# Three modulation vectors of a diffusion trunk: products on GpSimd and sums on ScalarE in place of TensorE matmuls

## The chip, the cores and the metric

One core of a Trainium2 chip runs the whole program. The metric is the device time of one execution in microseconds, smaller being better. The engines are TensorE (PE, with its weight loads PEld), VectorE (DVE), ScalarE (ACT), GpSimd (POOL) and SyncE (SP), which here only issues DMAs.

## What is computed

Two layers, each an FFN, a mixer (latent attention beside a state-space branch S5) and another FFN, on 256 latent and 256 context tokens of 1024 channels. Each branch is normed, scaled and shifted ahead, and gated behind, by vectors of 1024 channels that come from a conditioning vector: nine per layer, for the latent and for the context tokens.

```python
mod_x = (silu(c) @ ada_w[l] + ada_b[l]).reshape(B, 9, 1, 1024)
mod_c = (silu(c_ctx) @ ada_w[l] + ada_b[l]).reshape(1, 9, 1, 1024)
sublayer_in  = rmsnorm(h, g_pre) * (1 + mod[:, 3*s + 1]) + mod[:, 3*s]
sublayer_out = h + weight * mod[:, 3*s + 2] * rmsnorm(y, g_post)
# branch s: 0 first FFN, 1 mixer, 2 second FFN
```

Vector 2 of a layer is so the gate behind the first FFN; 3 and 4 are shift and scale ahead of the mixer.

## The kernel before

All matmuls of the main path are made of three in fp32r: a weight tile of 128x512 is loaded (`raw`), ScalarE rounds it (`whi`), VectorE subtracts (`wlo`), and TensorE multiplies whi and wlo with the high and low parts of the activations (`hhi`/`hlo` behind a norm, `hi`/`lo` behind a gate). The FFN goes through its 22 blocks of hidden channels in four segments; the last part of the last segment is done for the 256 context tokens first and the latent ones next (h = 0, 1), eight output blocks of 15 matmuls each. Behind every block `close` (line 765) makes x², (G y)² and x·G y into a tile `tri` for the statistics: the squares and `y` scaled by the gate on ScalarE, the product x·y on GpSimd for blocks 0 to 5 (on VectorE for 6 and 7). TensorE adds their columns (`misc<-tri`), `Norm.chain` (line 2036) makes the norm's factors on VectorE, TensorE spreads them (`acc<-sp`), and `Norm.block` (line 2065) gives hhi and hlo, for which ScalarE needs the shift `B` and the scale `A`.

Beside this path S5's matrices of the layer are built (`s5_build`, line 1599): mostly VectorE products of 128x512 (`P`, `mt`, ...), then small matmuls (`acc<-P,c`, transposes `acc<-ident,mt`), ScalarE copies (`m`, `kb`) and stores to DRAM issued by GpSimd (`stg`, `kd`).

The 18 vectors come in three ways. `ada_first` (line 838) makes vectors 0 and 1 of layer 0 at the start, on TensorE. `ada_gen` (line 791) makes 2, 3 and 4 of layer 0: for each half of a vector eight pieces of 128x512 of ada_w are loaded (`aw`), each multiplied by the two conditioning vectors (32 columns, four matmuls a piece), copied to a row (`adr`), transposed and added to the bias: 48 pieces. `ada_rows` (line 864) makes the other 13 on VectorE, from rows of the transposed ada_w: each 128x512 tile `ar` is multiplied by the conditioning vector on all partitions (`crow`) and summed in one instruction.

```python
for j in range(4):
    nc.tensor.matmul(bank[32 * j:32 * j + 32], self.silu[:, kt, :], w[:, j * 128:(j + 1) * 128],
                     start=kt == 0, stop=kt == 7)
```

The order of the work is not that of the code. The class Recorder takes down all instructions with a time at which each is due, and `schedule` (line 379) orders each engine's queue by its own estimates. Work beside the path is a "filler": `add_filler` (line 627) records one step whenever the recorded time of the main path passes its next due time; what is marked lazy is put into idle time up to then. `need` (line 892) records the rest of a generator at once when a vector is wanted that is not there. All instructions are issued from one line of `emit` (line 576), so every row of the trace has L576.

Of the kernel before, what the change touches and what calls it, by code (L numbers as in the profile page):

```python
# [17 lines left out]
L = 2  # L18
# [4 lines left out]
LEAD = 6  # L23
# [11 lines left out]
ADA_ROWS = [(0, 5), (0, 6), (0, 7), (0, 8), (1, 0), (1, 1), (1, 2), (1, 3), (1, 4), (1, 5), (1, 6), (1, 7), (1, 8)]  # L35
ROWS_FROM, ROWS_PACE = 360000.0, 4.5
# [8 lines left out]
ADA_PACE = 12000.0  # L45
# [27 lines left out]
class View:  # L73
    """A part of an on-chip tile, as strides over [128 partitions, columns]."""
# [55 lines left out]
    def extent(self):  # L130
        """The first partition, the last, and the columns as bits."""
        p, c = divmod(self.offset(), self.root.cols)
        key = c, self.arr.shape[1:], self.arr.strides[1:]
        if key not in MASKS:
            at = np.array([c])
            for n, st in zip(*key[1:]):
                at = (at[:, None] + st * np.arange(n if st else 1)).reshape(-1)
            m = 0
            for x in at.tolist():
                m |= 1 << x  # L140
            MASKS[key] = m
        return p, p + self.arr.shape[0], MASKS[key]
# [14 lines left out]
class Root:  # L157
    """A tile: lasting, or one of a tag's buffers from its first write to its last use."""
# [18 lines left out]
class Scratch:  # L177
    """A part of a DRAM tensor, with what tells it from parts that other instructions use."""
# [41 lines left out]
class Recorder:  # L220
    """Records instructions, then issues them in the order of a list schedule.

    An instruction waits for those that it depends on and for its buffers; each engine takes the one that was
    recorded for the earliest time among those that can run.
    """
# [18 lines left out]
    # ---------------------------------------------------------------- tiles  # L244
# [14 lines left out]
    # ---------------------------------------------------------------- priorities  # L259
    @contextmanager  # L260
    def aside(self, late, pace=0.0, lazy=False):
        """Work beside the main path, as if recorded some time later, and by and by.

        Lazy work is for an engine's idle time, up to the time at which its result is needed.
        """
# [8 lines left out]
    # ---------------------------------------------------------------- recording  # L274
    def cost(self, eng, method, a, kw):
        """Time on the engine, in ns."""
# [101 lines left out]
    # ---------------------------------------------------------------- schedule  # L378
# [166 lines left out]
    def lacks(self, op):  # L545
        """A tile that the instruction is the first to use and that has to wait for a buffer, if there is one.

        A tile gets a buffer only if all that is still to come, in the order of the recording, then fits as well.
        """
# [29 lines left out]
class Trunk:  # L579
# [24 lines left out]
    # ---------------------------------------------------------------- storage  # L604
# [21 lines left out]
    # ---------------------------------------------------------------- fillers  # L626
    def add_filler(self, gen, interval, delay=0.0, late=0, pace=0.0, lazy=False):
        """A generator whose steps are recorded at intervals, with the priority of a later time.

        With a pace the intervals are that many times VectorE's work in a step.  # L630
        """
# [21 lines left out]
    # ---------------------------------------------------------------- weights  # L653
# [8 lines left out]
    def wget(self):  # L662
        """Loads and splits the weights that come next."""
# [14 lines left out]
    # ---------------------------------------------------------------- matmuls  # L678
# [20 lines left out]
    # ---------------------------------------------------------------- norms  # L699
    def part(self, t, h):  # L700
        """Half h of the tokens of a tile: 0 the context, 1 the latent ones, which an x-only tile holds alone."""
# [10 lines left out]
    def stat(self, r, q, n=1):  # L712
        """Adds a block's column sums to n regions of the statistics bank: 4 quadrants by 64 tokens."""
# [5 lines left out]
    def rsqrt(self, v, plain=False, wide=True, times=1.0, mask=None):  # L719
        """times/sqrt of [quadrant, token] rows: as they are, and with the tokens of other quadrants as zeros."""  # L720
# [28 lines left out]
    def rstd(self, r, width, n=1):  # L749
        """1/rms of the sums of squares in n regions from r on."""  # L750
# [4 lines left out]
    def spread(self, p, rows):  # L755
        """Rows of 64 tokens, one of each quadrant, to [128, 256 tokens] on every partition."""
# [8 lines left out]
    def close(self, l, s, i, h, y, src, fast, last=False):  # L765
        """Statistics of half h of block i of a branch's output: sums of src^2, y^2 and x y for y = G src."""
# [21 lines left out]
    # ---------------------------------------------------------------- modulation  # L788
    ADA_AHEAD = 4

    def ada_gen(self, units):
        """One step: one [128, 512] piece of ada_w for the two conditioning vectors."""
        nc = self.nc
        halves = [(l, m, h) for l, m in units for h in range(2)]
        pieces = [(*x, kt) for x in halves for kt in range(8)]
        tiles = {}
        nxt = 0

        def load(upto):
            nonlocal nxt  # L800
            while nxt < min(upto, len(pieces)):
                l, m, h, kt = pieces[nxt]
                w = self.rec.tile("slot", 512, F32, "aw")
                c = m * 1024 + h * 512
                nc.sync.dma_start(w, self.io["ada_w"][l, kt * 128:(kt + 1) * 128, c:c + 512])
                tiles[nxt] = w
                nxt += 1

        tail = []

        def finish(l, m, h, row):
            tp = self.aux()[:, 0:128]
            nc.tensor.transpose(tp, row, self.ident)
            c = m * 8 + h * 4
            nc.vector.tensor_tensor(_ap(self.mods[l], c * 2, [[2, 4], [1, 2]]), _ap(tp, 0, [[32, 4], [1, 2]]),
                                    _ap(self.adab, l * 72 + c, [[1, 4], [0, 2]]), op=ALU.add)
            if h == 1:
                self.have[l, m] = True

        for i, (l, m, h, kt) in enumerate(pieces):  # L820
            load(i + 1)
            if kt == 2 and tail:
                finish(*tail.pop())
            w = tiles.pop(i)
            if kt == 0:
                bank = self.acc()[:, 0:128]
            for j in range(4):
                nc.tensor.matmul(bank[32 * j:32 * j + 32], self.silu[:, kt, :], w[:, j * 128:(j + 1) * 128],
                                 start=kt == 0, stop=kt == 7)
            if kt == 7:  # L830
                row = self.sm(128, tag="adr")
                nc.scalar.activation(row, bank, AF.Copy)
                tail.append((l, m, h, row))
            yield
        finish(*tail.pop())
        yield

    def ada_first(self):
        """One step: a quarter of the channels of the two units that the first norm needs."""
# [23 lines left out]

    def ada_rows(self, units):
        """The same on the vector engine: one step gives 128 channels from their rows of the transposed ada_w."""
# [79 lines left out]
    def fill_ada(self, n):  # L945
        for _ in range(n):
            if next(self.ada, 0) == 0:
                return
# [1264 lines left out]
```

## Time and profile before

| | us |
|---|---|
| median of 3 runs | 2319.44 (2319.03 to 2321.52) |
| span of the profiled execution | 2323.8 |
| TensorE busy | 2275.3 |
| VectorE busy | 1870.1 |
| ScalarE busy | 1029.1 |
| GpSimd busy | 300.6 |

The page lists for the profiled execution its span, from the first instruction to the last, and no separate device time; it lies 4.4 us above the median. The matmuls are pipelined, so a matmul's own duration is longer than the distance to the next one. The first FFN of layer 0 ends and its mixer begins between 461 and 468 us; the profile's windows are cut there.

### The profile page before, as it was taken

The numbers are of one execution on the slowest core, as the hardware profiler recorded it, in microseconds if no ns is written. First come the engines' busy times: TensorE is split into PE (matmuls) and PEld (weight loads), VectorE is DVE, ScalarE is ACT, GpSimd is POOL, SyncE is SP. The second block draws the span as 40 slices with busy tenths as digits, with TensorE's granted clock in tenths as the row PEclk, the third lists the DMA queues.
The fourth block names the chain that finished last, engine by engine and source line by source line (L and its number), as shares of the span: only waits on it lengthen the run. The fifth ranks groups of instructions, "written<-read, shape, count | busy, mean of one in ns | idle before, by whom it ended". The sixth has DMA issues, their size and how long they took to land. (4 is left out here: it accounts for less than half of the span.)

```text
span 2323.8 us, 43733 instructions
## 1 busy us (share of the span) xinstructions
PE 2275.3 (98%) x15768; PEld 1947.8 (84%) x15768; DVE 1870.1 (80%) x4313; ACT 1029.1 (44%) x2050; POOL 300.6 (13%) x455
## 2 busy tenths in 40 slices
PE   8999999999999999999999999999999999998998
PEld 6887878887888888898888888888889898897997
DVE  4997788889889889699997899898557678877554
ACT  5332233653246644543222463333246446575452
POOL 0010111430100200200100131100004110312000
PEclk9999999999999999999999999999999999998999
DMA  9354556966874546243564645656445795673562
GB/s 318 97 162 147 170 186 202 350 194 197 295 256 148 162 147 226 69 123 111 163 197 125 206 148 161 206 191 227 155 137 161 244 299 174 174 258 120 178 195 88
DMA packets 237481, 428.06 MB, mean 184 GB/s; under 512 B 29488, under 2 KB 58032, under 8 KB 237264
## 3 DMA queue, kind: packets, MB, share of 16 engines
q1 hardware_dynamic: 213904, 350.79, 47.8%
q0 software_dynamic: 23360, 74.48, 9.1%
q8 instruction: 124, 2.03, 0.4%
q14 instruction: 93, 0.76, 0.1%
HBM read 366.56 MB, written 58.59 MB: 183 GB/s over the span
## 5 line engine op out<-in xcount | busy, mean ns | idle before, releaser
L576 PE MATMUL acc<-hhi,whi 128*128 128x256 f32 (+2 forms) x2112 | 717.1, 345 | 4.8 <-ACT hhi L576 4.1
L576 PE MATMUL acc<-hhi,wlo 128*128 128x256 f32 (+2 forms) x2112 | 707.6, 343 | 0.0
L576 PE MATMUL acc<-hlo,whi 128*128 128x256 f32 (+2 forms) x2112 | 699.9, 342 | 1.5 <-DVE hlo L576 1.5
L576 ACT ACTIVATE whi<-raw 128x512 fp32r<-128x512 f32 x802 | 476.0, 623 | 367.1 <-PE acc L576 157.8
L576 DVE TENSOR_TENSOR wlo<-raw,whi 128x512 fp32r<-128x512 f32 x802 | 529.6, 686 | 125.4 <-ACT whi L576 75.8
L576 PEld LDWEIGHTS acc<-hhi,whi 128*128 128x128 f32 (+1 forms) x2112 | 398.8, 190 | 56.9 <-ACT hhi L576 6.7
L576 PEld LDWEIGHTS acc<-hhi,wlo 128*128 128x128 f32 (+1 forms) x2112 | 398.9, 190 | 47.5 <-issue 0.6
L576 PEld LDWEIGHTS acc<-hlo,whi 128*128 128x128 f32 (+1 forms) x2112 | 390.3, 189 | 50.8 <-DVE hlo L576 2.8
L576 PE MATMUL acc<-hi,whi 128*128 128x512 f32 (+1 forms) x1144 | 392.4, 345 | 1.5 <-ACT hi L576 1.5
L576 PE MATMUL acc<-lo,whi 128*128 128x512 f32 (+1 forms) x1144 | 389.0, 341 | 0.0
L576 PE MATMUL acc<-hi,wlo 128*128 128x512 f32 (+1 forms) x1144 | 378.8, 343 | 0.6 <-DVE wlo L576 0.6
L576 PEld LDWEIGHTS acc<-hi,whi 128*128 128x128 f32 x1144 | 215.3, 189 | 32.4 <-issue 5.1
L576 PEld LDWEIGHTS acc<-hi,wlo 128*128 128x128 f32 x1144 | 214.3, 189 | 27.6 <-DVE wlo L576 1.8
L576 PEld LDWEIGHTS acc<-lo,whi 128*128 128x128 f32 x1144 | 215.6, 189 | 24.6 <-issue 0.3
L576 ACT ACTIVATE sg<-acc 128x512 f32<-128x512 f32 (+1 forms) x129 | 64.8, 503 | 252.2 <-PE acc L576 234.3
L576 ACT ACTIVATE hi<-sg 128x512 fp32r<-128x512 f32 (+1 forms) x113 | 60.4, 540 | 158.1 <-DVE sg L576 129.6
L576 DVE TENSOR_TENSOR sg<-sg,acc 128x512 f32<-128x512 f32 (+1 forms) x97 | 55.6, 574 | 90.4 <-ACT sg L576 63.4
L576 POOL TENSOR_TENSOR tri<-x,y 128x256 f32<-128x256 f32 x54 | 54.7, 1018 | 323.5 <-ACT y L576 296.1
L576 DVE CUSTOM_DVE_ANT_0 ar<-ar,crow,adab 128x512 f32<-128x512 f32 x104 | 77.6, 750 | 4.5 <-DMA ar<-in_ada_t_dram 4.5
L576 DVE TENSOR_TENSOR lo<-sg,hi 128x512 fp32r<-128x512 f32 (+1 forms) x113 | 66.0, 589 | 17.5 <-ACT hi L576 9.9
L576 DVE CUSTOM_DVE_ANT_0 ar<-ar,crow,ah 128x512 f32<-128x512 f32 x104 | 78.8, 758 | 1.5 <-DMA ar<-in_ada_t_dram 0.9
L576 POOL DMA_DIRECT2D stg<-P x64 | 34.8, 543 | 345.1 <-DVE P L576 345.1
(249 smaller groups left out, 3282.2 us busy)
## 6 DMA issues: line engine op xcount, KB each, us to landing
raw<-in_w_gu_dram SPq DMA_DIRECT2D x352, 256.0 KB, 3.2
ar<-in_ada_t_dram SPq DMA_DIRECT2D x208, 256.0 KB, 3.4
raw<-in_w_dn_dram SPq DMA_DIRECT2D x176, 256.0 KB, 3.2
raw<-in_w_sq_dram SPq DMA_DIRECT2D x128, 256.0 KB, 4.6
raw<-in_w_in_dram SPq DMA_DIRECT2D x112, 256.0 KB, 4.9
m1l<-stg SPq DMA_DIRECT2D x96, 256.0 KB, 5.0
aw<-in_ada_w_dram SPq DMA_DIRECT2D x80, 256.0 KB, 5.8
stg<-P POOLq DMA_DIRECT2D x64, 256.0 KB, 3.8
```

The source lines that it names most:

```text
L576: getattr(getattr(self.tc.nc, engine), method)(*[real(v) for v in a], **{k: real(v) for k, v in kw.items()})
```

## The change

`ada_gen` goes, and `ada_sums` takes its place for the same three vectors. A step makes 128 channels: two tiles `ar` of 128x512 from the transposed ada_w, each multiplied on GpSimd by the `crow` of the two conditioning vectors, and each product summed along its row by a ScalarE copy with an accumulator (`apart`). After eight steps VectorE adds the halves and the bias. So there are 4 products and 4 sums a step, 24 steps. The first step is due at 25 us of the main path's recorded time, the others 14.5 us apart. The `crow` tiles are loaded by this generator, earlier than before. The rest of the diff takes comments out.

```diff
-ADA_PACE = 12000.0
+ADA_SUMS = [(0, 2), (0, 3), (0, 4)]
+SUMS_FROM, SUMS_PACE = 25000.0, 14500.0
...
+    def ada_sums(self, units):
+        nc = self.nc
+        self.load_crow()
+        for u, (l, m) in enumerate(units):
+            part = self.const([128, 32], name="apart")
+            for b in range(8):
+                w = [self.blk(name="ar") for _ in range(2)]
+                for i in range(2):
+                    nc.sync.dma_start(w[i], self.io["ada_t"][len(ADA_ROWS) + u, b, :, i * 512:i * 512 + 512])
+                for r in (0, 1):
+                    for i in range(2):
+                        o = self.blk(name="aj") if r == 0 else w[i]
+                        c = 4 * b + 2 * r + i
+                        nc.gpsimd.tensor_tensor(o, w[i], self.crow[r][i], op=ALU.mult)
+                        nc.scalar.activation(o, o, AF.Copy, accum_out=part[:, c:c + 1])
+                yield
+            v = self.modv(l, m)
+            q = part.rearrange("p (b i) -> p b i", i=2)
+            nc.vector.tensor_tensor(v, q[:, :, 0], q[:, :, 1], op=ALU.add)
+            o = v.rearrange("p (b r) -> p b r", r=2)
+            bias = self.adab[:, l * 72 + m * 8:l * 72 + m * 8 + 8].unsqueeze(2).to_broadcast([128, 8, 2])
+            nc.vector.tensor_tensor(o, o, bias, op=ALU.add)
+            self.have[l, m] = True
+            yield
...
-        self.ada = self.ada_gen([(l, m) for l in range(L) for m in range(9) if (l, m) not in ADA_ROWS + [(0, 0), (0, 1)]])
+        self.ada = self.ada_sums(ADA_SUMS)
...
-        self.add_filler(self.ada, ADA_PACE, 2000.0, LATE_A, 0.0, True)
+        self.add_filler(self.ada, SUMS_PACE, SUMS_FROM, LATE_A, 0.0, True)
```

How the queues move is read from the order of the built programs. The numbers behind the names tell tiles apart within one program alone. GpSimd at the end of the first FFN, before: the products x·y of blocks 3 (context), 0, 4, 5, 1 to 5, between stores of S5's matrices.

```order
L576 TENSOR_TENSOR tri_4839<-x_87,y_1778 128x256
L576 DMA kd_99<-kb_4893 128x240
L576 DMA stg_101<-m_4904 128x512
L576 DMA stg_101<-m_4917 128x512
L576 DMA stg_101<-m_4931 128x512
L576 DMA stg_101<-m_4942 128x512
L576 TENSOR_TENSOR tri_4992<-x_84,y_1641 128x256
L576 TENSOR_TENSOR tri_5051<-x_88,y_1813 128x256
L576 TENSOR_TENSOR tri_5079<-x_89,y_1842 128x256
L576 TENSOR_TENSOR tri_5161<-x_85,y_1690 128x256
```

The same place in the changed program begins with these rows; `aj` and `ar` are products with `crow`, and behind the last row of the piece 16 more of them follow, the last being ar_4808.

```order
L577 TENSOR_TENSOR aj_4790<-ar_4498,crow_115 128x512
L577 TENSOR_TENSOR tri_4781<-x_88,y_1931 128x256
L577 TENSOR_TENSOR aj_4838<-ar_4526,crow_114 128x512
L577 TENSOR_TENSOR aj_4859<-ar_4534,crow_115 128x512
L577 TENSOR_TENSOR ar_4526<-ar_4526,crow_112 128x512
L577 TENSOR_TENSOR ar_4534<-ar_4534,crow_113 128x512
```

Behind ar_4808 stands the product x·y of block 5 for the context tokens, tri_4788, and behind it the tri for the latent ones:

```order
L577 DMA kd_99<-kb_5231 128x240
L577 TENSOR_TENSOR tri_4788<-x_89,y_1967 128x256
L577 DMA stg_101<-m_5069 128x512
L577 DMA stg_101<-m_5114 128x512
L577 TENSOR_TENSOR tri_4947<-x_84,y_1734 128x256
```

Further on, behind the rest of the tri and two x of the norm, come stores, and at their end the 22nd product, the last of the three vectors:

```order
L577 DMA stg_101<-m_5425 128x512
L577 DMA stg_101<-m_4872 128x512
L577 DMA stg_101<-m_4883 128x512
L577 DMA kd_99<-kb_4901 128x240
L577 DMA stg_101<-m_5271 128x512
L577 TENSOR_TENSOR ar_4498<-ar_4498,crow_113 128x512
```

Twenty-two products have come into this part of the queue; tri_4788 stands behind 21 of them, and ar_4498 behind all the stores.

ScalarE at the mixer's first norm, before: two tri, the last whi, and the first hhi.

```order
L576 ACTIVATE tri_5391<-y_1918 128x256
L576 ACTIVATE tri_5391<-y_1918,cG_112 128x256
L576 ACTIVATE whi_5400<-raw_5076 128x512
L576 ACTIVATE hhi_5411<-pn_5398,c_75,cA_113 128x8x32
L576 ACTIVATE pn_5416<-pn_5398,c_75,cA_113 128x256
```

And in the changed program, where `apart` is the sums' tile:

```order
L577 ACTIVATE tri_5359<-y_1967 128x256
L577 ACTIVATE whi_5389<-raw_5146 128x512
L577 ACTIVATE whi_5397<-raw_5157 128x512
L577 ACTIVATE whi_5407<-raw_5167 128x512
L577 ACTIVATE whi_5418<-raw_5175 128x512
L577 ACTIVATE m_5425<-acc_5226 128x512
L577 ACTIVATE ar_4498,apart_118<-ar_4498 128x512
L577 ACTIVATE hhi_5503<-pn_5438,c_75,cA_120 128x8x32
```

The last sum has come to stand directly ahead of the first hhi.

## Rows read from the trace of the kernel before

**Rows 1.** The page, its first part: busy us, share of the span, instructions.
```profile
PE 2275.3 (98%) x15768; PEld 1947.8 (84%) x15768; DVE 1870.1 (80%) x4313; ACT 1029.1 (44%) x2050; POOL 300.6 (13%) x455
```

**Rows 2.** Windows: stretch, its length, busy us by engine, clock, DMA share, GB/s.
```profile
50.00:200.00 150.00, 150.00 (x742) 127.58 (x741) 137.90 (x361) 56.58 (x101) 10.82 (x20) 1.00 0.47 152
200.00:400.00 200.00, 199.80 (x1139) 159.91 (x1138) 161.44 (x274) 60.11 (x105) 23.72 (x44) 1.00 0.53 170
400.00:468.00 68.00, 65.61 (x758) 56.21 (x757) 58.84 (x142) 42.56 (x95) 26.34 (x38) 0.98 0.96 343
```

**Rows 3.** Windows of tile aw, of tile adr; TensorE's timeline around pieces of aw.
```profile
100.00:460.00 360.00, 20.35 (x384) 10.87 (x384) 1.00 0.59 196
...
100.00:460.00 360.00, 1.69 (x6) 0.84 (x6) 1.65 (x6) 1.00 0.59 196
...
421.22 1.52 PE L576 MATMUL acc<-aw,c 128*32 128x128 f32 x48
422.55 0.51 PE L576 MATMUL misc<-tri,c 128*32 128x192 f32 x8
...
436.01 0.29 PE L576 MATMUL acc<-lo,whi 128*128 128x256 f32 x1
436.23 0.42 PE L576 MATMUL acc<-aw,c 128*32 128x128 f32 x8
436.58 0.39 PE L576 MATMUL acc<-hi,wlo 128*128 128x256 f32 x1
```

**Rows 4.** ScalarE's groups by form: count, busy us, mean ns, idle before.
```profile
L576 ACT ACTIVATE whi<-raw 128x512 fp32r<-128x512 f32 x794 | 472.8, 625 | 367.1 <-PE acc L576 157.8 <-DMA raw<-in_w_gu_dram 45.8 <-DVE wlo L576 32.7
L576 ACT ACTIVATE tri<-y 128x256 f32<-128x256 f32 x102 | 40.8, 413 | 34.9 <-DVE y L576 22.4 <-PE misc L576 11.0 <-issue 0.3
L576 ACT ACTIVATE m<-acc 128x512 f32<-128x512 f32 x64 | 36.0, 595 | 29.2 <-PE acc L576 28.0 <-DVE wlo L576 0.8 <-DMA stg<-m 0.3
L576 ACT ACTIVATE y<-y,cG 128x256 f32<-128x256 f32 x48 | 23.6, 501 | 1.3 <-DVE tri L576 0.6
L576 ACT ACTIVATE tri<-y,cG 128x256 f32<-128x256 f32 x12 | 5.9, 493 | 0.0
L576 ACT ACTIVATION_READ_ACCUMULATOR sj<-acc 128x1 f32 x4 | 0.8, 193 | 0.0
```

**Rows 5.** GpSimd's groups; then tri alone, its shortest, median and longest.
```profile
L576 POOL TENSOR_TENSOR tri<-x,y 128x256 f32<-128x256 f32 x54 | 54.7, 1018 | 323.5 <-ACT y L576 296.1 <-issue 11.8 <-DVE y L576 5.2
L576 POOL DMA_DIRECT2D stg<-m x64 | 34.6, 543 | 114.0 <-ACT m L576 104.3 <-ACT kb L576 6.0 <-ACT y L576 2.0
...
L576 POOL TENSOR_TENSOR tri<-x,y x54: 722/752/6595, 418.9 to 2104.7; 128x256 f32<-128x256 f32 x54
```

**Rows 6.** TensorE's timeline: S5's transposes and products; the step into the mixer.
```profile
402.17 1.91 PE L576 MATMUL acc<-ident,mt 128*128 128x128 f32 x16
409.20 1.07 PE L576 MATMUL acc<-P,c 128*32 128x128 f32 x12
...
461.58 0.28 PE L576 MATMUL acc<-hi,wlo 128*128 128x256 f32 x1
...
464.02 0.48 PE L576 MATMUL misc<-tri,c 128*32 128x192 f32 x2 [1.37 <-DVE tri L576]
...
467.39 0.58 PE L576 MATMUL acc<-hhi,whi 128*128 128x256 f32 x1
```

**Rows 7.** Windows behind that wait; the granted clock stands third from the right.
```profile
466.00:467.00 1.00, 1.00 (x15) 0.63 (x14) 1.00 (x4) 0.97 (x2) 0.00 (x0) 0.50 1.22 199
...
468.00:469.00 1.00, 1.00 (x9) 1.00 (x9) 0.97 (x3) 1.00 (x4) 0.00 (x0) 0.82 0.17 36
```

**Rows 8.** Timelines of VectorE and of GpSimd where both multiply.
```profile
933.69 1.23 DVE L576 CUSTOM_DVE_ANT_0 ar<-ar,crow,adab 128x512 f32<-128x512 f32 x1
...
937.45 0.75 DVE L576 CUSTOM_DVE_ANT_0 ar<-ar,crow,adab 128x512 f32<-128x512 f32 x1
...
933.25 2.26 POOL L576 TENSOR_TENSOR tri<-x,y 128x256 f32<-128x256 f32 x2 [3.40 <-ACT y L576]
```

More of the change, by code (lines that the diff above doesn't have):

```diff
@@ L786, in close @@
         self.rec.pull = None
[L789 to L836, printed above, removed]
     def ada_first(self):
@@ L862, in ada_first, with load_crow @@
             yield
+    def load_crow(self):
+        nc = self.nc
+        self.crow = {}
+        for r in (1, 0):
+            self.crow[r] = [self.const([128, 512], name="crow") for _ in range(2)]
+            for i in range(2):
+                nc.sync.dma_start(self.crow[r][i], self.io["crow"][r, i].to_broadcast([128, 512]))
+                nc.scalar.activation(self.crow[r][i], self.crow[r][i], AF.Silu)
+    def ada_sums(self, units):
+        nc = self.nc
+        self.load_crow()
[6 more added lines that the diff above has]
+                for r in (0, 1):
+                    for i in range(2):
+                        o = self.blk(name="aj") if r == 0 else w[i]
[11 more added lines that the diff above has]
+            yield
     def ada_rows(self, units):
         nc = self.nc
-        cs = {}
-        for r in (1, 0):
-            cs[r] = [self.const([128, 512], name="crow") for _ in range(2)]
-            for i in range(2):
-                nc.sync.dma_start(cs[r][i], self.io["crow"][r, i].to_broadcast([128, 512]))
-                nc.scalar.activation(cs[r][i], cs[r][i], AF.Silu)
+        cs = self.crow
         for u, (l, m) in enumerate(units):
@@ L943, in lead @@
                 evac(h, j, bank)
[L945 to L948, printed above, removed]
     def gated(self, sg, pg, pu, out):
@@ L2131, in layout @@
     o["ada_w"] = a["ada_w"]
-    o["ada_t"] = np.stack([a["ada_w"][l][:, m * 1024:m * 1024 + 1024].T.reshape(8, 128, 1024) for l, m in ADA_ROWS])
+    o["ada_t"] = np.stack([a["ada_w"][l][:, m * 1024:m * 1024 + 1024].T.reshape(8, 128, 1024) for l, m in ADA_ROWS + ADA_SUMS])
     o["crow"] = np.stack([a["c_ctx"].reshape(2, 1, 512), a["c"][0].reshape(2, 1, 512)])
```

## The prediction

> **What bounds the kernel now.** I read the page's list of engines first: TensorE is busy for 2275.3 us of a span of 2323.8 us, so nearly every microsecond of its work is a microsecond of the program, and an edit elsewhere counts only where it makes TensorE wait or spares it work [rows 1]. The windows come next, cut at the places that the change touches. In 50 to 200 us TensorE never stops, and VectorE is busy for 137.90 of 150 us; in 200 to 400 us VectorE has 161.44 of 200; in 400 to 468 us, the end of the first FFN and the step into the mixer, TensorE still has 65.61 of 68 us while ScalarE has 42.56 and GpSimd 26.34 [rows 2]. So in these 418 us TensorE is the bound with VectorE close behind, and ScalarE and GpSimd have room on the average. The end of this stretch is a special place: the last matmul of the first FFN starts at 461.58, and the mixer's first matmul, which needs the norm and the modulation vectors 3 and 4, at 467.39. The 5.8 us between hold statistics, spreads and one wait of 1.37 us [rows 6].
>
> **What goes.** The 48 pieces of ada_w leave, with 192 matmuls, which the trace has as 384 records in 100 to 460 us with 20.35 us of TensorE, and six transposes with 1.69 us together [rows 3]. That is an upper end of 22.0 us, since neighbours overlap in it. A lower end comes from the timeline: six pieces in a row take from 421.22 to 422.55, 0.22 us each, so 48 take 10.6; a piece alone pushes the matmul behind it from about 436.13 (the one before started at 436.01, 0.12 apart) to 436.58, 0.45 us each, so 48 take 21.6 [rows 3]. Most stand in small groups, many among other 32-column products that hide a part of their change of shape. I take **18 us less on TensorE**, with 16 and 22 as its ends. All of it lay on the bound. The six copies to rows on ScalarE and six small additions on VectorE go too, and six small additions on VectorE come: nothing. The DMAs are the same in number and size, 48 of 128x512 numbers, and only come from the transposed rows; I cost them at nothing, since the windows' share of the DMA engines is half or less except in 400 to 468 us, where fewer of them now fall [rows 2].
>
> **What comes.** 96 products of 128x512 on GpSimd and 96 sums on ScalarE. By the order, 36 products stand together ahead of GpSimd's first store, 38 more are spread among its stores, and 22 stand in the last piece, shown above: from aj_4790 to ar_4498.
>
> *The step into the mixer.* Here the hiding ends. The first hhi of the mixer needs the scale and shift, these need the last sum (ar_4498, the row just ahead of it on ScalarE), and that its product, the last of the 22 on GpSimd. From the multiplication tri_4788 on ScalarE to that hhi stand 84 instructions: 22 sums, 14 whi, 19 tri squares, 12 y, 11 m, 4 tri with the coefficient and 2 kb. A sum is priced as a whi at 0.625, plus reading the accumulator at 0.193: 0.82 us. With rows 4 that is 22 x 0.82 = 18.0, 14 x 0.625 = 8.8, 19 x 0.413 = 7.8, 12 x 0.501 = 6.0, 11 x 0.595 = 6.5, 4 x 0.493 = 2.0 and some 0.7 for the kb: **49.8 us of ScalarE** [rows 4]. GpSimd in the same stretch has 22 products, 8 tri and 2 x (10 at the 0.752 median) and 12 issues of DMAs at 0.543: 14 us and 22 products. A 128x512 product is nowhere in the trace. ScalarE's step from 128x256 to 128x512 is 0.413 to 0.625, half as much again; so I bound a product from below by 1.5 x 0.752 = 1.13 us, and from above by twice the mean of the 256-wide ones, 2 x 1.018 = 2.04 [rows 4, 5]: 39 to 59 us in all, 62 with the ten others at their mean too. TensorE in the same stretch has 143 matmuls of the FFN at 0.12, 31 transposes at 1.91/16, 24 products of P (48 records at about 0.07) and 12 small ones of tri: 17.2 + 3.7 + 3.4 and under 1 for the last = 25 us [rows 6]. So ScalarE alone ends 24.8 us after TensorE's last FFN matmul, where it was 5.8: **+19 us**. GpSimd by its ends, with 2.5 us for the last sum and the coefficients, gives +11 to +33. I keep ScalarE's value, which all comes from rows of the same instructions. A wait of this length also costs clock: after the 1.37 us wait the granted clock was 0.50 (1.2 GHz) in 466 to 467 and 0.82 in the third microsecond after [rows 7]; **+1.5 us**, 0 to 2.
>
> *VectorE beside GpSimd.* The trace shows the two in each other's way. With GpSimd idle one of VectorE's custom products takes 0.75 us; at 933.69, with two GpSimd products of 128x256 running (2.26 us for both, where 0.752 is the median of one), it took 1.23 [rows 5, 8]. That is 0.48 us lost on VectorE by one 256-wide product, and 0.48 to 0.96 for a 512-wide one; I take 0.7. The first 36 fall where VectorE is 92% busy: 36 x 0.7 x 0.92 = 23 us, of which its 12 idle us in 50 to 200 take the half: **+11 us** for TensorE, which waits for the split weights (wlo) behind these delays; 0 to 33. The 38 in the middle meet a VectorE that is 81% busy with 38.6 idle us: 38 x 0.7 x 0.81 = 21.5, and I let less than a half through, **+9 us**, 0 to 29 [rows 2].
>
> The Trainium skill, GPSIMD Engine Reference, section "Key points", says the same of the place: GpSimd shares its SBUF interfaces with VectorE, and they contend where a VectorE instruction has two SBUF inputs. The trace agrees, with the 0.48 us. [...]
>
> **The sum**: -18 + 19 + 1.5 + 11 + 9 = +22.5 us on the profiled execution, whose span of 2323.8 us lies 4.4 above the median of the three runs. Put on the median, 2319.4 + 22.5 = **2342 us**, slower by 1.0%. What a measurement of this kernel can tell from no change is about 0.2%, 4.6 us.
>
> **Rivals.**
> *Faster: the sums fit beside the matmuls.* It decides at the step: if GpSimd's last 22 products and ScalarE's sums run ahead of the FFN's end, so that the step costs under 13 us in place of 19, and VectorE's idle time takes all of the contention, the 18 us win. With GpSimd at its lower end: -18 + 11 = -7, with 22 removed -11: about 2310. For it: ScalarE and GpSimd are idle for more than half of 50 to 400 us [rows 2]. Against it: ScalarE's 49.8 us are made of measured rows and stand in one queue.
> *No change: the step eats the gain.* All of the step and none of the contention: -18 + 19 + 1.5, about 2322.
> *VectorE becomes the bound.* If every product holds it for 0.96 us, 74 products ahead of the last piece cost 71 us; with the 50.7 idle us of rows 2 only half usable that leaves 46, and with -18 + 20.5 some 2367; with the step at GpSimd's upper end 2380. For it: the 0.48 at half the width. Against it: operations that read an accumulator bank need not collide.
> *The change does not do what it says*, since the pace leaves five blocks of the last unit to be called in one go: the order shows exactly that, and it is inside my term of the step.
>
> **How the numbers follow.** The forecast (2325 to 2360) has 0.50, VectorE as the bound (over 2360) 0.24, no change 0.13, faster 0.13. The bounds added up give -22 + 11 = -11 at one end and -16 + 33 + 2 + 33 + 29 = +81 at the other; both ends of all terms at once are unlikely, so the range is 2310 to 2382, with about one in ten left out on each side. Faster by over 0.2% 0.13, within 0.2% 0.12, slower 0.75.
>
> **What would show it.** Right: the matmuls on aw end near 40 us; GpSimd's products of 128x512 average 1.2 to 1.8 us; the wlo beside them are longer than 0.69; in the step TensorE idles for some 15 to 25 us, with ScalarE and GpSimd nearly full, and the mixer starts near 490 us instead of 467. Each term has its own place: the difference up to about 200 us, up to 400 us, and at the step. Wrong: if the mixer starts before 467 the step or the contention was oversized; if TensorE does not wait there, the queues were ahead; and if the difference arises after the mixer has begun, the reasoning has missed a cause altogether.

## The result, and the profile after

The changed kernel takes 2392.53 us (median of 4 runs, 2389.57 to 2394.69), where the kernel before takes 2320.02 beside it: a ratio of 1.0308, 95% interval 1.0294 to 1.0323, slower by 72.5 us. The forecast was 2342, its range ended at 2382. The direction was right; the loss is three times the forecast one.

The page's list of engines after, with a span of 2391.6 us, answers to [rows 1].

```profile
PE 2281.4 (95%) x15378; PEld 1947.8 (81%) x15378; DVE 1957.4 (82%) x4313; ACT 1090.2 (46%) x2236; POOL 446.8 (19%) x551
```

VectorE has the same 4313 instructions and is busy for 87 us more. The windows at the places of [rows 2], and behind them the stretch that now holds the step into the mixer (stretch, length, busy us by engine, granted clock, DMA share, GB/s):

```profile
50.00:200.00 150.00, 130.40 (x611) 108.54 (x611) 147.09 (x314) 71.86 (x166) 62.01 (x48) 0.93 0.41 137
200.00:400.00 200.00, 186.28 (x906) 150.79 (x906) 180.16 (x267) 73.61 (x152) 67.07 (x75) 0.97 0.51 169
400.00:468.00 68.00, 61.10 (x368) 50.29 (x367) 62.78 (x95) 28.91 (x63) 25.15 (x25) 0.97 0.50 164
468.00:560.00 92.00, 60.96 (x497) 53.06 (x496) 80.72 (x179) 58.42 (x144) 59.07 (x60) 0.81 0.49 167
```

Already in 50 to 200 us TensorE stops for 20 us, and VectorE, at 147.09 of 150, does 314 instructions where it did 361. TensorE's waits in 60 to 200 us have one kind (total, times, longest):

```profile
PE acc L577 <- DVE wlo L577: 19.6, 6, 6.6
```

What makes the split weights late is seen where GpSimd multiplies without a pause. VectorE's timeline (start, us, instruction):

```profile
144.38 0.40 DVE L577 TENSOR_TENSOR xi<-xi,xt 128x128 f32<-128x128 f32 x1
144.68 1.27 DVE L577 COPY fr<-ta 128x64 f32<-128x64 f32 x1
145.84 1.35 DVE L577 COPY fi<-ta 128x64 f32<-128x64 f32 x1
147.08 1.49 DVE L577 TENSOR_TENSOR xt<-xi 128x192 f32<-128x192 f32 x1
148.50 1.44 DVE L577 TENSOR_TENSOR xi<-xr,xi 128x192 f32<-128x192 f32 x1
149.86 1.42 DVE L577 TENSOR_TENSOR xr<-xr,xt 128x192 f32<-128x192 f32 x1
151.21 1.41 DVE L577 TENSOR_TENSOR xt<-xi,xr 128x192 f32<-128x192 f32 x1
152.54 1.33 DVE L577 TENSOR_TENSOR fr<-fr 128x64 f32<-128x64 f32 x1
153.79 1.42 DVE L577 TENSOR_TENSOR xi<-xi,xt 128x192 f32<-128x192 f32 x1
155.13 0.47 DVE L577 TENSOR_SCALAR xr<-xr,sgn 128x512 f32<-128x512 f32 x1
```

and GpSimd's in the same us, the third row ending at 155.00:

```profile
143.62 3.48 POOL L577 TENSOR_TENSOR aj<-ar,crow 128x512 f32<-128x512 f32 x2 [3.84 <-issue]
147.06 2.66 POOL L577 TENSOR_TENSOR ar<-ar,crow 128x512 f32<-128x512 f32 x2
...
152.37 2.63 POOL L577 TENSOR_TENSOR ar<-ar,crow 128x512 f32<-128x512 f32 x2
```

With the row left out, two more of the kind, these are eight products, and beside them eight VectorE instructions, each as long as a product, whether it has 64 columns or 192. In the trace of before one of these copies took:

```profile
117.82 0.23 DVE L576 COPY fi<-ta 128x64 f32<-128x64 f32 x1
```

So here the two engines go one for one, and VectorE pays about 1.1 us for each of these turns, where the prediction had 0.48 to 0.96 for a product; over all 96 products it is 0.88 (below). When the products stop, the next instruction of 512 columns takes 0.47. The Trainium skill, SBUF — State Buffer, section "Who interferes with whom", bears on this: a VectorE instruction with two SBUF inputs, and copies or scalar operations in a two-port mode, contend with GpSimd for a shared pair of ports, which whoever comes first keeps for the whole instruction. The two copies of 1.27 and 1.35 us agree with it.

TensorE waits for the wlo that stands behind these eight, and then works at a lower granted clock for some us: 0.50, that is 1.2 GHz, in 156 to 160 us. Its timeline, with rows left out:

```profile
156.86 0.79 PE L577 MATMUL acc<-hi,wlo 128*128 128x512 f32 x1 [6.57 <-DVE wlo L577]
...
158.30 0.63 PE L577 MATMUL acc<-hi,wlo 128*128 128x512 f32 x1
158.73 0.63 PE L577 MATMUL acc<-hi,whi 128*128 128x512 f32 x1
...
161.48 0.40 PE L577 MATMUL acc<-lo,whi 128*128 128x512 f32 x1
161.72 0.39 PE L577 MATMUL acc<-hi,wlo 128*128 128x512 f32 x1
```

The matmuls start 0.43 us apart at first and 0.24 us apart three microseconds later.

**Where the time arises.** The three traces compared here (before, after, and the first experiment) have 3536 matmuls that read a wlo, in the same sequence. The start of the k-th, less its start in the kernel before:

```
k (start before, us)     200 (140.8)  550 (420.7)  600 (453.6)  625 (471.1)  1000 (813.0)  last (2314.9)
changed kernel               +29.1        +30.2        +48.2        +75.6         +75.0          +67.8
products of 32 columns        -1.0        -25.9        -25.3         +0.5          -0.1           -5.3
their difference              30.1         56.1         73.5         75.1          75.1           73.1
```

The second line is the first experiment, the changed kernel with short products. The windows up to k = 200 and from there to k = 550, of the changed kernel and then of the one with short products, show what the difference is made of:

```profile
60.00:169.90 109.90, 90.30 (x395) 73.58 (x394) 109.31 (x245) 50.08 (x126) 56.05 (x37) 0.91 0.28 92
169.90:450.90 281.00, 263.69 (x1277) 214.63 (x1276) 258.39 (x385) 105.41 (x213) 88.49 (x101) 0.98 0.52 173
```

```profile
60.00:139.80 79.80, 79.80 (x388) 67.55 (x387) 78.68 (x252) 50.87 (x126) 26.92 (x39) 1.00 0.42 134
139.80:394.80 255.00, 255.00 (x1276) 211.84 (x1275) 222.22 (x382) 105.46 (x217) 55.92 (x101) 1.00 0.58 193
```

For the same work, up to a few matmuls at the edges, TensorE stands still for 19.6 and 17.3 us, where with short products it never stops, and is busy 10.5 and 8.7 us longer, at a granted clock of 0.91 and 0.98 in place of 1.00. Over the whole program it has the same 15378 instructions in both and is busy 24.8 us longer (2281.4 and 2256.6); the other 48.3 of the 73.1 us between the spans (2391.6 and 2318.5) are waits. Of the longer work some 17 us go by the clock, an estimate from its mean over the runs, 0.981 and 0.988: 0.007 of 2392 us. What the rest of it is stays open.

Everything is lost before the mixer runs; the last few us that come back belong to both kernels and were not looked into.

### The profile page after: what moved, and what is told of

Same layout as the page of the kernel before. It is cut to its first block, busy times and chain, and to the rows that moved or that the text cites. A ratio compares the mean times of both kernels' runs of the same rounds, so it can differ in the third digit from the quotient of the medians.

```text
span 2391.6 us, 43250 instructions
## 1 busy us (share of the span) xinstructions
PE 2281.4 (95%) x15378; PEld 1947.8 (81%) x15378; DVE 1957.4 (82%) x4313; ACT 1090.2 (46%) x2236; POOL 446.8 (19%) x551
## 5 line engine op out<-in xcount | busy, mean ns | idle before, releaser
L577 PE MATMUL acc<-hhi,wlo 128*128 128x256 f32 (+2 forms) x2112 | 715.7, 345 | 19.6 <-DVE wlo L577 19.6
L577 PE MATMUL acc<-hlo,whi 128*128 128x256 f32 (+2 forms) x2112 | 708.1, 344 | 1.4 <-DVE hlo L577 1.3
L577 DVE TENSOR_TENSOR wlo<-raw,whi 128x512 fp32r<-128x512 f32 x802 | 545.2, 707 | 106.1 <-ACT whi L577 77.1
L577 PE MATMUL acc<-hi,wlo 128*128 128x512 f32 (+1 forms) x1144 | 390.7, 346 | 23.2 <-DVE wlo L577 23.1
L577 POOL TENSOR_TENSOR aj<-ar,crow 128x512 f32<-128x512 f32 x48 | 76.0, 1592 | 164.1 <-DVE ta L577 66.1
```

The costliest lines, as they stand in the source:

```text
L577: getattr(getattr(self.tc.nc, engine), method)(*[real(v) for v in a], **{k: real(v) for k, v in kw.items()})
```

## The experiments

T1 is the taking of turns between GpSimd and VectorE, T2 ScalarE's queue with the sums in it, T3 the new order of the other instructions.

**1. Products, sums and order apart.** The order of the changed kernel is kept; where an instruction is issued, it is exchanged or left out (where the sums are left out, three memsets come in). The lines of the three edits that matter, with the runs that have them behind the #:

```diff
+            if op.kind == "product":              # e_short, e_order
+                a = [v[:, 0:32] for v in a]
+            if op.kind == "sum":                  # e_short
+                a = [a[0], self.plain, *a[2:]]
+            if op.kind == "sum":                  # e_nosums, e_order
+                continue
```

e_short: 

> The changed kernel with every instruction in its order; only the 96 products on GpSimd work on 32 of their 512 columns, and the 96 sums on ScalarE read a constant tile of the same size and still write the product's tile, so that they wait as they did. The three vectors (0,2), (0,3), (0,4) are not computed. T1 (GpSimd and VectorE take turns: VectorE loses about as long as a product lasts, at every place where the planner's slack is spent): without long products the +72 us goes, and what is left is the sums on ScalarE less the removed matmuls: 2310 to 2335. T2 (the sums stand in ScalarE's queue ahead of the high halves of the weights, with or without long products): stays above 2370. T3 (the new order itself, in which the first norm of the mixer stands behind the last vector and the second half's chain of VectorE): stays above 2355.

e_nosums: 

> The changed kernel with every instruction in its order; only the 96 sums on ScalarE are left out (the sums are set to zero ahead, so the three vectors are not computed and nothing waits for the last product). T1: the products still hold VectorE, so most of the loss stays: 2365 to 2390. T2: without the sums 78 us of ScalarE and its queue are free, and the time falls to 2300 to 2330. T3: the wait of the mixer's first norm for the last sum goes, the order stays: 2375 to 2385.

e_order: 

> The changed kernel's order with products of 32 columns and without the sums: what is left is the order of all other instructions, the loads of the transposed rows, and the removal of 192 matmuls and 6 transposes from TensorE. The three vectors are not computed. T1 with my -18 us for the removal: 2298 to 2310. T2: the same as T1 here, 2300 to 2310. T3: the order costs by itself, 2345 or more.

Measured: e_short 2319.99 us, ratio to before 0.9994 (0.9984 to 1.0003); e_nosums 2392.92, 1.0309 (1.0294 to 1.0324); e_order 2320.24, 0.9995 (0.9986 to 1.0004). The sums cost nothing: with or without them the time is the same, once with full and once with short products. T2 falls. The long products cost 72.5 us, all of the loss, as T1 says; e_nosums lies just above T1's 2390. But e_order, with nothing left but the order and the removal, was to gain 18 us and gains none: it misses T1's 2298 to 2310, and T3's 2345 as well. The order costs what the removal gains, and no more. The table above says where: the kernel is 25 us ahead at k = 600 and level at 625.

A rival for the 72.5 us is GpSimd's own queue, in which the products stand ahead of its products x·y (tri); short products relieve that queue too. The traces speak against it: from 60 us to k = 625 TensorE waits 42.7 us for wlo in the changed kernel, which no instruction of GpSimd makes, and 3.2 us for a tri of GpSimd; with short products it is nothing and 1.8 us.

That place in e_order, the step into the mixer. TensorE's timeline, those rows of 440 to 470 us ahead of which it waits:

```profile
445.06 2.81 PE L583 MATMUL misc<-tri,c 128*32 128x192 f32 x26 [6.91 <-DVE rs L583]
452.07 0.53 PE L583 MATMUL misc<-tri,c 128*32 128x192 f32 x8 [0.73 <-POOL tri L583]
455.33 1.19 PE L583 MATMUL acc<-sp,c 128*128 128x256 f32 x2 [2.72 <-DVE rs L583]
461.69 1.19 PE L583 MATMUL acc<-sp,c 128*128 128x256 f32 x2 [5.17 <-DVE rs L583]
466.91 1.22 PE L583 MATMUL acc<-sp,c 128*128 128x256 f32 x2 [4.03 <-DVE sp L583]
```

ScalarE's, at the mixer's first hhi:

```profile
453.85 0.57 ACT L583 ACTIVATE m<-acc 128x512 f32<-128x512 f32 x1
466.34 1.58 ACT L583 ACTIVATE hhi<-pn,c,cA 128x256 fp32r<-128x256 f32 x3 [11.92 <-DVE cA L583]
```

TensorE waits for VectorE, which computes the norm of both halves of the tokens (rs, sp), one after the other; the coefficients (cA) of the mixer's norm stand behind both. From 440 to 480 us TensorE is busy for 22.29 us at a granted clock of 0.66, where the kernel before has 37.63 at 0.96. In the kernel before the second half's chain began behind the first hhi, and was hidden under the mixer's matmuls; its first hhi and, on VectorE, the first row of that chain:

```profile
466.53 0.60 ACT L576 ACTIVATE hhi<-pn,c,cA 128x256 fp32r<-128x256 f32 x1
```

```profile
467.52 0.23 DVE L576 TENSOR_SCALAR rs<-misc 128x64 f32<-128x64 f32 x1
```

A part of the first wait, of 6.91 us, looks like the taking of turns again, with work that the kernel before has too; no run takes it apart. In e_order GpSimd makes four products x·y in one go, and beside them VectorE's custom product takes 1.88 us, where it takes 0.75 with GpSimd idle [rows 8]; the norm of the first half begins behind it:

```profile
438.63 3.22 POOL L583 TENSOR_TENSOR tri<-x,y 128x256 f32<-128x256 f32 x4
```

```profile
440.52 1.88 DVE L583 CUSTOM_DVE_ANT_0 aj<-ar,crow,adab 128x512 f32<-128x512 f32 x1
```

**2. The removal by itself, planned anew**: the loop with loads, products and sums is taken out of the generator.

```diff
-                w = [self.blk(name="ar") for _ in range(2)]
...
-                        nc.scalar.activation(o, o, AF.Copy, accum_out=part[:, c:c + 1])
```

> The changed kernel without loads, products and sums of the three vectors (they are the biases alone), planned anew: the removal of 192 matmuls and 6 transposes by itself. If the removal is worth the 16 to 22 us that the prediction took: 2298 to 2304. If the matmuls lay in time in which TensorE would have waited anyway: 2312 to 2322.

Measured: 2342.41 us, 1.0091 (1.0076 to 1.0106): less work, and slower than before, outside both ranges. The planner makes another order, and loses 20 us at a place of its own: k = 300 is 1.7 us early, 325, at 230 us, 18.5 late. So an order alone can cost this kernel some 20 us, and more where it also takes back the removal's gain.

**3. An earlier last vector.** The planner's pace of the three vectors, and its twin with short products.

```diff
-SUMS_FROM, SUMS_PACE = 25000.0, 14500.0
+SUMS_FROM, SUMS_PACE = 25000.0, 9000.0
```

e_pace: 

> The changed kernel with the steps of the three vectors recorded every 9 us in place of every 14.5 us, so that the last sum is planned near 240 us and the mixer's first norm has its coefficients long before it needs them. T3 (two losses: the products hold VectorE for some 73 us in all, and the order at the start of the mixer, where the last vector comes late, gives back the 26 us that the removed matmuls saved): the second goes, 2355 to 2375. If the time at the mixer's start comes with the removal whatever the order: 2385 to 2400. The planner may move other work too; it moved a plan without any of the sums by 22 us, and so much is the uncertainty of both.

e_pace_short: 

> The kernel with steps every 9 us, its order kept, with products of 32 columns (sums as long as they were, over a constant tile; the three vectors are not computed). T3: neither loss is left, only the removal's gain of about 25 us: 2290 to 2302. If the gain goes at the mixer's start whatever the order: 2315 to 2325. The difference to the run with full products is what VectorE's turns with GpSimd cost under this order: 60 to 90 us by T1.

Measured: e_pace 2387.32 us, 1.0286 (1.0267 to 1.0305), above T3's range; e_pace_short 2302.31, 0.9916 (0.9901 to 0.9931), level with its upper end. By its time alone e_pace fits the other reading (2385 to 2400, the step costs the removal's gain in any order); its twin with short products shows that it is not that. In this order the loss at the mixer's start is 7.5 us (37.5 ahead at k = 600, 30.0 at 625) in place of 26, and most of the removal's gain is kept: 17.6 us below before. But the products cost 85 us in it, 12 more than in the slower pace, and take it all back.

**4. What a product costs by its length and inputs.** Products of 256 columns, and copies of 512 with one input, both in the changed kernel's order.

```diff
+                a = [v[:, 0:256] for v in a]                        # e_half
+                method, a, kw = "tensor_copy", a[:2], {}            # e_copy
```

e_half: 

> The changed kernel in its order, with products of 256 in place of 512 columns (sums as long as they were, over a constant tile; the three vectors are not computed). At 32 columns the loss of 72 us was gone. If VectorE loses in proportion to how long a product lasts: half, 2350 to 2362. If it loses by the number of products, once they are longer than the neighbours: above 2370. If there is a length that VectorE's slack takes in: below 2340.

e_copy: 

> The changed kernel in its order, with the 96 products replaced by copies of the same 512 columns on GpSimd, one input in place of two (sums as long as they were, over a constant tile; the three vectors are not computed). If any GpSimd instruction of this length takes turns with VectorE: 2350 to 2395, in proportion to how long a copy lasts. If it is the two inputs that do it: 2318 to 2325, and VectorE's instructions beside a copy keep their lengths.

Measured: e_half 2345.78 us, 1.0104 (1.0090 to 1.0118); e_copy 2335.09, 1.0057 (1.0043 to 1.0071). Both fall between the ranges expected. Copies collide too, so a second input of GpSimd is not needed. In e_copy, the first row here stands beside the second of two copies, the last row has GpSimd idle:

```profile
103.50 1.50 POOL L583 COPY aj<-ar 128x512 f32<-128x512 f32 x2 [7.13 <-DVE lc L583]
```

```profile
104.45 0.68 DVE L583 TENSOR_TENSOR lc<-lc,ph 128x64 f32<-128x64 f32 x1
...
107.41 0.27 DVE L583 TENSOR_TENSOR lc<-lc,w 128x64 f32<-128x64 f32 x1
```

The loss grows with the length of GpSimd's instruction, faster than in proportion: 15, 26 and 72.5 us for medians of 0.78, 0.90 and 1.46. The groups of GpSimd (shortest, median, longest ns), in the changed kernel, then e_half, then e_copy:

```profile
L577 POOL TENSOR_TENSOR aj<-ar,crow x48: 1264/1461/3550, 66.5 to 504.8; 128x512 f32<-128x512 f32 x48
```

```profile
L583 POOL TENSOR_TENSOR aj<-ar,crow x48: 722/900/5767, 68.6 to 455.5; 128x256 f32<-128x256 f32 x48
```

```profile
L583 POOL COPY aj<-ar x48: 610/780/4402, 62.0 to 443.4; 128x512 f32<-128x512 f32 x48
```

**5. Product and sum on VectorE.** First planned anew, as the later vectors have it (e_rows), then in the very order of the changed kernel, each product exchanged where it is issued (e_swap).

```diff
-                        nc.gpsimd.tensor_tensor(o, w[i], self.crow[r][i], op=ALU.mult)
-                        nc.scalar.activation(o, o, AF.Copy, accum_out=part[:, c:c + 1])
+                        nc.vector.tensor_tensor_reduce(o, w[i], self.crow[r][i], op0=ALU.mult, op1=ALU.add,
+                                                       scale=1.0, scalar=0.0, accum_out=part[:, c:c + 1])
```

e_rows: 

> The changed kernel with products and sums of the three vectors in one instruction on VectorE (96 of 0.75 us and as many reads of 0.08 us, as the later vectors have it) in place of GpSimd and ScalarE, planned anew. T1 (what a product on GpSimd costs is VectorE's time, 0.76 us passed on for each): VectorE's own 80 us cost about the same, 2365 to 2400. If it is the taking of turns by two engines that costs, and not VectorE's share: below 2345.

e_swap: 

> The changed kernel with every other instruction in its order; each product on GpSimd and its sum on ScalarE are issued as one instruction on VectorE (0.69 us and a read of 0.08 us) at the product's place. The same order takes 2392.5 us with products on GpSimd and 2320.0 us with short ones. If the loss is VectorE's time, 0.76 us passed on for each product: 2385 to 2395. If it is the taking of turns, in which VectorE's small instructions each last as long as a product: 2320 to 2350.

Measured: e_rows 2337.71 us, 1.0072 (1.0056 to 1.0089), in the range for turns; e_swap 2353.11, 1.0135 (1.0121 to 1.0149), just above the range for turns and far below the other. The same product costs 33 us on VectorE itself and 72.5 us on GpSimd, in one and the same order; VectorE is busy 0.54 us longer for each on itself, and 0.88 us for each beside GpSimd. So T1 falls where it says that VectorE's time by itself is the price, and stands as the taking of turns. The page's list of engines, e_short and then e_swap:

```profile
PE 2256.6 (97%) x15378; PEld 1934.9 (83%) x15378; DVE 1872.9 (81%) x4313; ACT 1085.8 (47%) x2236; POOL 356.0 (15%) x551
```

```profile
PE 2269.6 (97%) x15378; PEld 1938.2 (82%) x15378; DVE 1924.6 (82%) x4505; ACT 1029.5 (44%) x2044; POOL 300.8 (13%) x455
```

With VectorE's busy time against e_short the five kernels of one order stand in a row:

| in the changed kernel's order | time, us | above e_short | VectorE busy above e_short | passed on |
|---|---|---|---|---|
| copies of 512 on GpSimd | 2335.1 | 15.1 | 27.6 | 0.55 |
| products of 256 on GpSimd | 2345.8 | 25.8 | 36.1 | 0.71 |
| product and sum on VectorE | 2353.1 | 33.1 | 51.7 | 0.64 |
| products of 512 on GpSimd | 2392.5 | 72.5 | 84.5 | 0.86 |

Of the three with GpSimd, the one that holds VectorE more passes a larger part on: the first 28 us lose a half, the last 48 us (36.1 to 84.5) lose 47. The clock has a share in this. TensorE is busy 5.0, 5.5 and 24.8 us longer than in e_short with copies, products of 256 and products of 512, and its waits alone, the rest of the spans' differences, are 0.39, 0.50 and 0.57 of what VectorE is held.

**6. The exchange at other paces**, as in 5 in the order with products on GpSimd and steps every 9 and 11 us.

e_swap9: 

> The same exchange in the order with steps every 9 us, which takes 2387.3 us with products on GpSimd and 2302.3 us with short ones. VectorE's time: 2375 to 2390. Taking of turns: 2302 to 2330, perhaps faster than the kernel before.

e_swap11: 

> The same exchange in the order with steps every 11 us; the last vector is planned near 290 us. Taking of turns: 2302 to 2330, as with 9 us, with less work of the three vectors in any stretch. VectorE's time: 2375 to 2390.

Measured: e_swap9 2334.46 us, 1.0056 (1.0044 to 1.0069), just above the range for turns; e_swap11 2335.15, 1.0057 (1.0043 to 1.0071), above it as well. With 9 us the exchange saves 53 of the 85 us. Neither beats before.

**7. The late coefficients.** In e_order, the ten VectorE instructions that make vector 4 and the scale of the mixer's first norm are issued earlier.

```diff
+        early = [op for op in ops if op.kind == "coef"]
+        at = max(i for i, op in enumerate(ops) if op.kind == "third")
+        for op in rest(ops[:at + 1]) + early + rest(ops[at + 1:]):
```

> The order of the changed kernel with products of 32 columns and without the sums (2320.2 us), in which the ten small VectorE instructions that make the vector (0,4) and the coefficients of the mixer's first norm are issued right behind the vector (0,3), some 60 us earlier; the three vectors are not computed. There the first norm on ScalarE waited 11.9 us for the coefficients, 8.7 us of it after its input was there (457.6 to 466.3 us). If that wait is what the order costs at the mixer's start: 2307 to 2314. If the rest of the chain (the second half's statistics ahead of it on VectorE) is as late without it: 2317 to 2323.

Measured: 2320.01 us, 0.9996 (0.9987 to 1.0005): not the gain of the first range, but the second, in which the rest of the chain is as late without it. The wait went, and stood one instruction later; ScalarE's timeline in e_early:

```profile
458.98 1.58 ACT L587 ACTIVATE hhi<-pn,c,cA 128x256 fp32r<-128x256 f32 x3 [2.60 <-DVE pn L587]
469.76 0.60 ACT L587 ACTIVATE pn<-pn,c,cA 128x256 f32<-128x256 f32 x1 [9.20 <-PE acc L587]
```

The three hhi go 9.3 us earlier, counting that all in this run is 1.9 us later, and the next instruction waits for a matmul of the second half's spread (sp), which stands ahead of the mixer in TensorE's queue. The whole order there was made around a late vector; moving the coefficients alone does not unmake it.

**8. Versions that might beat both.** Product and sum on VectorE planned anew at four paces, and the kernel before with its pieces of ada_w by fours.

```diff
-SUMS_FROM, SUMS_PACE = 25000.0, 14500.0
+SUMS_FROM, SUMS_PACE = 25000.0, 9000.0       # e_rows9; 7000, 11000, 12500 in the others
```

```diff
-            yield                             # e_group
+            if kt % 4 == 3:
+                yield
...
-ADA_PACE = 12000.0
+ADA_PACE = 48000.0
```

e_rows9: 

> Products and sums of the three vectors in one instruction on VectorE, as in the run that took 2337.7 us, and their steps every 9 us in place of every 14.5 us. There the 91 instructions between 50 and 440 us let TensorE run without a stop and were 30 us ahead of the kernel before at 443 us; all of the loss came after, where the last instructions, at 480 us, held back the coefficients of the mixer's first norm. T4 (VectorE has room for its own instructions, and only turns with GpSimd and the late last vector cost): the vectors are done near 250 us and nothing is late: 2295 to 2312, faster than before. If VectorE has no room at this density: 2320 to 2345.

e_rows7: 

> The same with steps every 7 us: the products are denser, 5 us of VectorE's work in every 7 us of planned time being theirs in part (four instructions, 3.1 us). T4: as with 9 us, 2295 to 2312. If VectorE's room ends with the density: slower than the one with 9 us by 5 to 30 us.

e_rows11: 

> Products and sums in one instruction on VectorE, planned anew, with steps every 11 us (2337.7 us with 14.5, 2321.3 with 9, 2336.6 with 7). If the late last vector and the density are two losses with a pace between them that has neither: 2298 to 2314. If each pace gives the planner another order whose losses have no trend: anything from 2315 to 2340.

e_rows12: 

> The same with steps every 12.5 us. Two losses with a pace between them: 2300 to 2318. No trend: 2315 to 2345.

e_group: 

> The kernel before with the pieces of the three vectors recorded by fours, every 48 us, in place of one every 12 us. A lone piece holds TensorE 0.35 to 0.45 us in the trace of before, pieces in a row 0.22 us: if that holds, 48 pieces save up to 8 us, 2311 to 2318; if the order of the rest moves, anything within 20 us.

Measured: e_rows9 2321.30 us, 1.0000 (0.9991 to 1.0009); e_rows7 2336.59, 1.0064; e_rows11 2342.26, 1.0084; e_rows12 2335.82, 1.0061; e_group 2322.68, 1.0007 (0.9997 to 1.0016). None beats the kernel before: e_rows9 is as fast, e_rows11 lies outside both of its ranges, and e_group does not save its up to 8 us. The paces have no trend: 7, 9, 11, 12.5 and 14.5 us give 2337, 2321, 2342, 2336, 2338. The account of two losses with a pace between them falls; each pace is another order.

## Why the prediction was wrong

*What goes: -18.* Right in size. At k = 600 the kernel with short products is 25.3 us ahead; by then it has run 16 of S5's products and 8 of its transposes fewer than before, about 2 us of them by the prediction's 0.07 and 0.12 us each, so some 23, just above the upper end of 22. In the order of e_pace_short 17.6 us stay to the end. In the changed kernel's own order nothing stays.

*VectorE beside GpSimd: +11 and +9.* **This is the step that failed most**: the place and the mechanism were right, the size was not. Measured, +30 up to k = 200 for 36 products and +26 up to 550 for the next 37. One factor was too small, one was nearly right, and a term was missing. A product was taken to cost VectorE 0.7 us times its busy share, 0.57 to 0.64; VectorE's busy time rose by 0.88 us for each of the 96 (84.5 us). Half of it or less was to be let through as waits, because VectorE had 12 and 38.6 idle us; TensorE waited for 19.6 us of 36 x 0.88 = 32, and for 17.3 of 37 x 0.88 = 33, so that this factor was not far off. What was missing is the clock: the sum has it at the step alone and at nothing here, and the same matmuls took 10.5 and 8.7 us longer in these two stretches, at a granted clock of 0.91 and 0.98; by the clock alone it would be 0.09 x 109.9 = 10 and 0.02 x 281 = 6 us, an estimate. All in all 0.86 of what VectorE was held, over the 96, came through. The price came from one custom instruction beside one 256-wide pair, and was scaled by the product's width; in the stretch without a pause, the instructions that pay are small ones of 0.2 to 0.4 us, and each pays the whole product.

*The step: +19 and +1.5.* The step cost 45.4 us (30.2 behind at k = 550, 75.6 at 625), and the reason given was wrong. ScalarE's queue of 49.8 us did not decide: without the sums, 18 us of it, the time is the same. In its place stand two things that the sum had at zero: the turns of the last 23 products, 19 us (56.1 to 75.1), and 26 us of order (25.9 and 25.3 ahead, then 0.5 behind), the norms of both halves ahead of the mixer's first matmul. The +1.5 for the clock was too little as well: the granted clock from k = 600 to 625 is 0.70, and 0.68 with short products, where before has 0.90. The order did show the last sum directly ahead of the first hhi; what else had moved there was not read.

*What would show it.* GpSimd's products average 1.53 us (76.0 and 70.8 us for 48 each), as bounded; the wlo of 50 to 200 us average 795 ns; the mixer's k = 625 starts at 546.7 where before had 471.1, not some 23 us later. In those 44.9 us from k = 600 TensorE stands still for 22.0, within the 15 to 25 us forecast for the step, but this was luck: ScalarE is busy for 27.4 of them and GpSimd for 28.9, not nearly full, and 19.7 us of the waits are for VectorE's rs and sp. All of the difference arises at the three places named.

*The rivals.* "VectorE becomes the bound" was nearest, with 2367 to 2380 at 0.24: it had the 0.96 us for each product that the trace now nearly bears out, and still took half of the idle time off.

*Left open*: which part of the order at the mixer's start (the second half's chain on VectorE, its spreads on TensorE, the buffers) has to move for the 26 us to go, since e_early moved the coefficients alone and e_pace_short changes the whole plan; and why the pace of 9 us makes the products dearer by 12 us.

## What to carry to other kernels

Work put on GpSimd beside a busy VectorE is to be priced as VectorE's time, and not as free because GpSimd is idle: here 0.88 us for each product of 1.53 us on the average, and some 1.1 us where GpSimd multiplies without a pause, whatever the size of what VectorE does next to it. Where TensorE is the bound, the time at a lower granted clock behind the waits comes on top, here some 17 of 73 us by the estimate above. Here VectorE could do product and sum itself for less than half the price. An order made by a planner is a part of the change: exchange instructions in a fixed order to find what they cost, and give a newly planned order an uncertainty of its own, here 20 us and more.

## What had not been expected of the hardware

A COPY of 64 columns, with one input, took 1.27 and 1.35 us beside products, where it takes 0.23 without; and a copy on GpSimd, 0.61 us at its shortest, holds VectorE too, if less (27.6 us for 96 copies, 84.5 for 96 products). A sum of 512 numbers on ScalarE with its accumulator (0.62 and 0.19 us, 96 of them) cost the program nothing at all, beside TensorE and in a queue with the weights.
